# Four x tiles of an SSD group in one slot, and one POOL add of [128, 4, 128] where there were four of [128, 128]

## The chip, the core and the metric

The kernel runs on one NeuronCore of a Trainium2 chip. The metric is the device time of one execution in microseconds; the time quoted is the median of three runs. A profiled execution gives the trace, whose span starts at its first and ends at its last recorded instruction.

PE is the matmul engine (TensorE), DVE the vector engine, ACT the scalar engine, POOL the GpSimd engine; SP issues most DMAs. Each runs its own instructions strictly in order and waits on semaphores for the others.

## The reference, cut to what matters

One layer over 1024 rows of 1024 features: an RMS norm, a projection into eight parts, a gated MLP branch, a Mamba-2 branch (SSD), a merge, and an embedding stage. The change lies in the SSD branch, whose y is made of three parts:

```python
xs, bm, cm = jnp.split(silu(conv(xbc)), ...)            # x: 32 heads of 64; 4 groups of B and C
y_diag = einsum('bclsg,bclsgr,bcsgrp->bclgrp', CB, Lmat, Xdt)     # inside a chunk of 128 rows
y_off  = einsum('bcgrpn,bclgn,bclgr->bclgrp', prev, Cc, exp(dA_cs)) # from the state before the chunk
y = y_diag + y_off + X * d_skip
y_b = gated_group_rms_norm(y, z_b, ssm_norm_g)          # per group of 8 heads
```

## The kernel before

Everything is held transposed: features on partitions, the 1024 sequence positions along the free axis. Products that need fp32 accuracy are split into a high and a low part, so that a projection tile of 128 features (`in_proj`, by `mm3`, L107) is 48 matmuls of 128x512 into one of two PSUM slots `ps_...`.

The SSD branch runs over four groups of 8 heads. For a group, `group_in` makes the tiles B, C and four x tiles `cv_xs` by `conv_tile`: the projection, an ACT copy to SBUF (L343), three convolution steps on DVE that read the projection's PSUM slot (L346; the third one frees it), a tanh (L349) and a product (L350). Then come 8 chunks of 128 positions, `ssd_chunk`. In a chunk POOL fetches the decay rows (`lm`, L365), PE makes `pbc` and the transposes `pxt`; ACT turns `lm` into a decay matrix (L400, L401), DVE multiplies it by `cbm` (L402) and makes `xdt` and `dx` (L382, L386); ACT and POOL split `dx` into `dxh` (L391) and `dxl` (L392). PE then makes `pyd` (inside the chunk, L407), `pyo` (from the state, L412, from the second chunk on) and the new state `pst` (L425 to L427), which POOL and DVE add to the old one (L433, L436). DVE scales `pyo` into `ex` (L415), and for each of the four x tiles DVE forms x*d + `pyd` in place (L417), to which POOL adds `ex` (L420).

While the chunks of a group run, PE fills the time with the projections of the group's four z tiles (`zb`) and of the next group's B, C and x. After the last chunk `group_out` multiplies x by z on DVE (L449), squares on ACT (L450), sums three times (L454, on POOL except in the last group), splits the sum into `qa` (ACT, L458) and `qb` (POOL, L459), sums over partitions on PE (`pn`, L462 and L463) and scales x by the resulting `rs` on DVE (L467); four DMAs store it. `t_sums` (L480 to L484) puts eight POOL operations for a later stage behind four of the chunks. After the group loop the `ga` projections begin, opened by five matmuls `wipe` (L528).

The order of instructions is set by the Tile scheduler when the kernel is built: it lays the work out by its own simulated times, and a pool hands a new tile the slot that is free first. All tiles of [128, 1024] of this stage (the eight normalised input tiles `x0`, then B, C, x, z, `qa`, `qb`) are from one pool `big` of 15 slots (L62). So a change in the pools or in the length of an operation can move work on every engine.

Of the kernel before, what the change touches and what calls it, by code (L numbers as in the profile page):

```python
# [8 lines left out]
F32 = mybir.dt.float32  # L9
F32R = mybir.dt.float32r  # L10
AF = mybir.ActivationFunctionType
ALU = mybir.AluOpType

P = 128
S = 1024
D = 1024
# [8 lines left out]
O_U, O_V, O_ZA, O_ZB, O_XS, O_B, O_C, O_DT, O_GA, O_GB = (  # L25
    0, 1024, 2048, 3072, 5120, 7168, 7680, 8192, 8224, 9248)
# [3 lines left out]
def kernel(  # L30
# [8 lines left out]
    nc = tc.nc  # L39
# [13 lines left out]
    def phase_pool(name, bufs):  # L53
        return pools.enter_context(tc.tile_pool(name=name, bufs=bufs, reuse_waits="tile"))

    def phase_banks(name, bufs):
        return banks.enter_context(tc.tile_pool(name=name, bufs=bufs, reuse_waits="tile",
                                                space=bass.MemoryType.PSUM))

    t2 = phase_pool("t2", 2)  # L60
    small = phase_pool("small", 2)
    big = phase_pool("big", 15)  # L62
    pss = phase_banks("pss", 4)
    pmm = phase_banks("pmm", 2)

# [80 lines left out]
    rstd0 = const.tile([P, NCH], F32, name="rstd0")  # L146
    xt = []
    for t in range(NCH):
        xv = big.tile([P, D], F32, tag="big", name=f"x0_{t}")
        nc.sync.dma_start(out=xv, in_=x[t * P:(t + 1) * P, :])  # L150
        xt.append(xv)

# [16 lines left out]
    def vec(nm, i):  # L169
        c = offs[nm] + i  # L170
        return vT[:, c:c + 1]

    def cw(k, i):
        return cwT[:, k * 24 + i:k * 24 + i + 1]
# [21 lines left out]
    for hf in range(2):  # L196
# [13 lines left out]
        for k in range(KD):  # L210
            pt = ps_ss(f"pt0_{hf}_{k}")
            for i in range(4):
# [4 lines left out]
                in1=hhi[k][hf].bitcast(F32), op0=ALU.mult, op1=ALU.subtract)  # L217
# [24 lines left out]
    def in_proj(name, col):  # L242
        w = proj_w(name, col)
        ps = ps_mm(f"ps_{name}")
        for k in range(KD):
            hi, lo = w[k // 4]
            mm3(ps, hi[:, k % 4, :], lo[:, k % 4, :], hhi[k], hlo[k], k == 0, k == KD - 1)
        return flat(ps)
# [54 lines left out]
    for n in (15, 13, 11, 9, 7, 5, 3):  # L303
# [7 lines left out]
        in1=abc.unsqueeze(1).broadcast_to([P, NCH, NH]), op0=ALU.mult, op1=ALU.mult)  # L311
# [24 lines left out]
    tad = dram.tile([D, S], F32, name="tad")  # L336
    tbd = dram.tile([D, S], F32, name="tbd")

    def conv_tile(name, col, ci):

        ps = in_proj(name, col)
        a = big.tile([P, S], F32, tag="big", name=f"cv_{name}")
        act(a, ps, AF.Identity, scale=cw(3, ci), bias=vec("cb", ci))  # L343
        for k in (2, 1, 0):
            sh = 3 - k
            stt(out=a[:, sh:], in0=ps[:, :S - sh], scalar=cw(k, ci), in1=a[:, sh:],  # L346
                op0=ALU.mult, op1=ALU.add)
        th = t4.tile([P, S], F32, tag="t4", name=f"th_{name}")
        act(th, a, AF.Tanh, scale=0.5)  # L349
        stt(out=a, in0=th, scalar=1.0, in1=a, op0=ALU.add, op1=ALU.mult)  # L350
        return a

    def group_in(g):
        bT = conv_tile(f"B{g}", O_B + g * P, 16 + g)
        cT = conv_tile(f"C{g}", O_C + g * P, 20 + g)
        xs = [conv_tile(f"xs{g}_{j}", O_XS + (4 * g + j) * P, 4 * g + j) for j in range(4)]
        return xs, bT, cT

    def ssd_chunk(g, c, xs, bT, cT, hst):
        n = f"{g}_{c}"  # L360
        cl = slice(c * P, (c + 1) * P)
        hs = slice(g * HG, (g + 1) * HG)
# [16 lines left out]
        for j in range(4):  # L379
# [3 lines left out]
           in1=dth[:, c, hs].unsqueeze(2).broadcast_to([P, HG, HD]), op=ALU.mult)  # L383
        if not last:
            dx = t2.tile([P, HG, HD], F32, tag="dx", name=f"dx_{n}", bufs=1)
            tt(out=dx, in0=pxt.rearrange("s (r d) -> s r d", d=HD),  # L386
               in1=dec4[:, c, hs].unsqueeze(2).broadcast_to([P, HG, HD]), op=ALU.mult)
# [6 lines left out]
        if c > 0:  # L394
            ex = t2.tile([P, 4, P], F32, tag="ex", name=f"ex_{n}")
# [20 lines left out]
        for j in range(4):  # L416
            stt(out=xs[j][:, cl], in0=xs[j][:, cl], scalar=dcol[:, 4 * g + j:4 * g + j + 1],  # L417
                in1=pyd[:, j * P:(j + 1) * P], op0=ALU.mult, op1=ALU.add)
            if c > 0:
                nc.gpsimd.tensor_tensor(out=xs[j][:, cl], in0=xs[j][:, cl], in1=ex[:, j, :], op=ALU.add)  # L420

        if last:
            return None
# [8 lines left out]
        else:  # L432
            nc.gpsimd.tensor_tensor(out=hn, in0=hst,  # L433
                                    in1=cdec[:, c, hs].unsqueeze(2).broadcast_to([P, HG, HD]),
                                    op=ALU.mult)
# [3 lines left out]
    def z_tile(g, j):  # L439
        ps = in_proj(f"zb{g}_{j}", O_ZB + (4 * g + j) * P)  # L440
        a = big.tile([P, S], F32, tag="big", name=f"zb{g}_{j}")
        act(a, ps, AF.Tanh, scale=0.5)
        stt(out=a, in0=a, scalar=1.0, in1=ps, op0=ALU.add, op1=ALU.mult)
        return a
# [30 lines left out]
    def t_sums(k):  # L475
        a = t4.tile([P, S], F32, tag="t4", name=f"ta{k}")
        b = t4.tile([P, S], F32, tag="t4", name=f"tb{k}")
        b11, b12, b21, b22 = a[:, 0:512], a[:, 512:1024], b[:, 0:512], b[:, 512:1024]
        for o_, kk, h in ((b11, k, 0), (b12, k, 1), (b22, k + 4, 1), (b21, k + 4, 0)):
            ptt(out=o_, in0=hhi[kk][h].bitcast(F32), in1=hlo[kk][h].bitcast(F32), op=ALU.add)  # L480
        ptt(out=b11, in0=b12, in1=b11, op=ALU.subtract)
        ptt(out=b12, in0=b22, in1=b12, op=ALU.subtract)
        ptt(out=b22, in0=b22, in1=b11, op=ALU.subtract)
        ptt(out=b21, in0=b21, in1=b22, op=ALU.subtract)  # L484
        nc.sync.dma_start(out=td[k, 0], in_=a)
        nc.sync.dma_start(out=td[k, 1], in_=b)
# [7 lines left out]

    t_when = {(0, 4): 0, (1, 1): 1, (1, 5): 2, (2, 2): 3}
    cur = group_in(0)
    for g in range(G):
        xs, bT, cT = cur
        hst = None
        for c in range(NCH):  # L500
            hst = ssd_chunk(g, c, xs, bT, cT, hst)
            if (g, c) in t_when:
                t_sums(t_when[g, c])
        zs = [z_tile(g, j) for j in range(4)]
        if g + 1 < G:
            cur = group_in(g + 1)
            group_out(g, xs, zs)
# [9 lines left out]
    for j in range(2):  # L517
        ps = in_proj(f"ga{j}", O_GA + j * P)
        a = t4.tile([P, S], F32, tag="t4", name=f"ga{j}")
# [227 lines left out]
    def y_slots(pi, k, i):  # L747
        if pi == 0:
            return [g2.tile([P, 512], F32R, tag="T", name=f"y{i}0_{k}_{h}", bufs=24) for h in range(2)]
        if pi == 1:  # L750
            return [hp_.tile([P, 512], F32R, tag="hB", name=f"y{i}1_{k}_{h}") for h in range(2)]
        return two(big.tile([P, S], F32R, tag="big", name=f"y{i}{pi}_{k}"))

    for pi, (src, w, kp) in enumerate(parts):
        yh, yl = [], []
        if pi == 1:
# [3 lines left out]
            big = phase_pool("big", 15)  # L760
        for k in range(4):
# [3 lines left out]
            a, b = y_slots(pi, k, "h"), y_slots(pi, k, "l")  # L765
# [153 lines left out]
```

## Time and profile before

| | us |
|---|---|
| median of 3 runs (1490.16 to 1494.23) | 1493.08 |
| the profiled execution | 1492.43 |
| its span | 1490.7 |
| PE busy in the span | 1457.2 |
| DVE / ACT / POOL busy | 821.2 / 677.8 / 641.4 |

The span is 1.73 us shorter than the profiled execution's own time. By the trace, group 0's projections begin at about 50 us, the SSD chunks of the four groups run from 112 to 645 us, the `ga` tiles to 690, the pairs of projections of the gated branch to 1040, the output projections to 1390, and the embedding stage to the end. "Busy" of PE counts pipelined matmuls, which start some 0.23 us apart and last longer than that each; a bracket behind a row of a timeline gives the time for which the engine had nothing to run before it, and who released it.

### The profile page before, as it was taken

Reading aid. Unit: us, or ns where it says so; the run is one execution under the profiler, and the core shown is the slowest. Engines: PE = TensorE matmul, PEld = TensorE weight load, DVE = VectorE, ACT = ScalarE, POOL = GpSimd, SP = SyncE. Lnnn points to the kernel's source line nnn. Section 1 sums busy time; section 2 is a strip of 40 time slices with the busy share of each in tenths; the row PEclk is TensorE's granted clock in tenths of the full one; section 3 lists DMA queues with packets and bytes.
Section 4 is the critical chain, followed back from the end, with each engine's and each line's share of the span. In section 5 each row is a group of like instructions: output and inputs, shape, how many; then the busy total and the mean of one; then the engine's idle time right before and its main releaser. Section 6 shows DMA issues by size and latency. Waiting matters only on the chain.

```text
span 1490.7 us, 19028 instructions
## 1 busy us (share of the span) xinstructions
PE 1457.2 (98%) x7109; PEld 1199.7 (80%) x7109; DVE 821.2 (55%) x1214; ACT 677.8 (45%) x1216; POOL 641.4 (43%) x605
## 2 busy tenths in 40 slices
PE   6999999999999999999999999999999999999997
PEld 5788888778878888778888888888888888888885
DVE  5454566767666765575337646444133566932554
ACT  6453655365555645546444434344422221421544
POOL 1226555965686655645443445454332333100110
PEclk9999999999999999999999999999999999999999
DMA  8322222432142223235434242244432465633641
GB/s 279 109 75 84 73 84 57 132 110 86 57 142 85 71 77 108 86 136 196 128 106 134 87 134 83 74 128 148 131 118 98 142 207 166 196 122 127 226 184 57
DMA packets 134273, 180.42 MB, mean 121 GB/s; under 512 B 7348, under 2 KB 101764, under 8 KB 134180
## 3 DMA queue, kind: packets, MB, share of 16 engines
q1 hardware_dynamic: 116624, 116.54, 24.7%
q0 software_dynamic: 16464, 59.43, 11.8%
q10 hardware_dynamic: 1092, 3.23, 0.6%
q8 instruction: 56, 0.92, 0.3%
q14 instruction: 37, 0.30, 0.1%
HBM read 137.10 MB, written 42.07 MB: 120 GB/s over the span
## 4 chain that ended last, share of the span: by engine, by line
PE 88%; POOL 4%; DMA 2%; ACT 2%; issue 2%; DVE 1%; SPq 0%; DVEq 0%; ACTq 0%; POOLq 0%
PE po L107 18%; PE ps_xs L107 12%; PE ps_zb L107 8%; PE px L107 6%; PE ppg L107 6%; PE x_v L610 3%; PE ps_C L107 3%; PE x_za L610 3%; PE ps_ga L107 3%; PE x_u L610 3%; PE x_gb L610 3%; PE ps_B L107 2%; DMA lm<-csd 2%; PE pyd L407 2%; PE pyo L412 2%
## 5 line engine op out<-in xcount | busy, mean ns | idle before, releaser
L107 PE MATMUL po<-yh,hi_o 128*128 128x512 f32 x384 | 149.4, 389 | 0.0
L107 PE MATMUL po<-yl,hi_o 128*128 128x512 f32 x384 | 149.4, 389 | 0.0
L107 PE MATMUL po<-yh,lo_o 128*128 128x512 f32 x384 | 118.6, 389 | 0.0
L232 POOL TENSOR_TENSOR lo_o<-raw_o,hi_o 128x512 fp32r<-128x512 f32 x48 | 63.1, 1317 | 114.0 <-ACT hi_o L231 110.7
L107 PE MATMUL ps_zb<-hhi,hi_zb 128*128 128x512 f32 x256 | 101.1, 395 | 0.0
L107 PE MATMUL ps_zb<-hlo,hi_zb 128*128 128x512 f32 x256 | 100.8, 394 | 0.0
L107 PE MATMUL ps_xs<-hhi,hi_xs 128*128 128x512 f32 x256 | 100.6, 393 | 0.0
L107 PE MATMUL ps_xs<-hlo,hi_xs 128*128 128x512 f32 x256 | 100.2, 391 | 0.0
L420 POOL TENSOR_TENSOR cv_xs<-cv_xs,ex 128x128 f32<-128x128 f32 x112 | 78.6, 729 | 35.0 <-DVE ex L415 33.0
L231 ACT CAST hi_o<-raw_o 128x512 fp32r<-128x512 f32 x48 | 29.6, 622 | 135.5 <-PE po L107 108.4
L107 PEld LDWEIGHTS po<-yh,lo_o 128*128 128x128 f32 x384 | 72.1, 188 | 15.1
L107 PEld LDWEIGHTS po<-yh,hi_o 128*128 128x128 f32 x384 | 72.1, 188 | 14.9
L107 PEld LDWEIGHTS po<-yl,hi_o 128*128 128x128 f32 x384 | 72.0, 188 | 14.9
L400 ACT ACTIVATE lm<-lm,cs 128x128 f32<-128x128 f32 x256 | 79.4, 390 | 9.8 <-DMA lm<-csd 9.2
L107 PE MATMUL ps_zb<-hhi,lo_zb 128*128 128x512 f32 x256 | 81.4, 397 | 0.0
L346 DVE SCALAR_TENSOR_TENSOR cv_xs<-ps_xs,cwT,cv_xs 128x1023 f32<-128x1023 f32 (+2 forms) x48 | 61.5, 1281 | 35.0 <-ACT cv_xs L343 34.0
L107 PE MATMUL ps_xs<-hhi,lo_xs 128*128 128x512 f32 x256 | 79.3, 391 | 0.0
L398 ACT ACTIVATE ex<-lm 64x512 f32<-64x512 f32 x56 | 35.3, 630 | 93.4 <-DMA lm<-csd 55.5
L232 POOL TENSOR_TENSOR lo_zb<-raw_zb,hi_zb 128x512 fp32r<-128x512 f32 x32 | 48.6, 1519 | 58.6 <-ACT hi_zb L231 58.6
L792 DVE TENSOR_TENSOR m<-m,po 128x512 f32<-128x512 f32 x48 | 30.8, 684 | 64.0 <-PE po L107 63.9
L232 POOL TENSOR_TENSOR lo_xs<-raw_xs,hi_xs 128x512 fp32r<-128x512 f32 x32 | 42.5, 1329 | 54.4 <-ACT hi_xs L231 52.7
L768 DVE TENSOR_TENSOR yl<-yraw,yh 128x512 fp32r<-128x512 f32 x48 | 35.7, 778 | 45.6 <-ACT yh L767 44.2
(519 smaller groups left out, 4023.9 us busy)
## 6 DMA issues: line engine op xcount, KB each, us to landing
lm<-csd POOLq DMA_DIRECT2D x32, 512.0 KB, 4.1
raw_xs<-in_w_in_dram SPq DMA_DIRECT2D x16, 512.0 KB, 4.0
raw_zb<-in_w_in_dram SPq DMA_DIRECT2D x16, 512.0 KB, 4.1
ybd<-cv_xs SPq DMA_DIRECT2D x16, 512.0 KB, 3.0
yraw<-ybd POOLq DMA_DIRECT2D x16, 512.0 KB, 3.8
raw_o<-in_w_ob_dram SPq DMA_DIRECT2D x16, 512.0 KB, 3.5
gt<-tad POOLq DMA_DIRECT2D x16, 512.0 KB, 4.5
x<-in_x_dram SPq DMA_DIRECT2D x8, 512.0 KB, 7.5
```

Source lines behind the costliest of these rows:

```text
L107: nc.tensor.matmul(o_, lhsT=a, rhs=b[h], start=(first and h not in seen), stop=(last and cnt[h] == 3))
L231: nc.scalar.copy(out=hi, in_=raw)
L232: (lo_on or nc.gpsimd.tensor_tensor)(out=lo, in0=raw, in1=hi.bitcast(F32), op=ALU.subtract)
L346: stt(out=a[:, sh:], in0=ps[:, :S - sh], scalar=cw(k, ci), in1=a[:, sh:], op0=ALU.mult, op1=ALU.add)
L398: act(ex[h * HD:(h + 1) * HD], lv[h * HD:(h + 1) * HD, :, h, :], AF.Exp)
L400: act(lm[:, r_, :], lm[:, r_, :], AF.Relu, bias=cs[:, c, g * HG + r_:g * HG + r_ + 1], scale=-1.0)
L407: nc.tensor.matmul(pyd[h * HD:(h + 1) * HD, (r_ // 2) * P:(r_ // 2 + 1) * P], lhsT=xdt[:, r_, :], rhs=lm[:, r_, :], start=True, stop=True)
L412: nc.tensor.matmul(pyo[:, j * P:(j + 1) * P], lhsT=hst[:, 2 * j:2 * j + 2, :].rearrange("s r d -> s (r d)"), rhs=cT[:, cl], start=True, st ...
L420: nc.gpsimd.tensor_tensor(out=xs[j][:, cl], in0=xs[j][:, cl], in1=ex[:, j, :], op=ALU.add)
L610: nc.tensor.matmul(pst, lhsT=l_[:, k, :], rhs=r_, start=(first and k == 0 and n_ == 0), stop=(k == 3 and n_ == 2), skip_group_check=True)
L768: tt(out=b[h], in0=raw[:, hsl[h]], in1=a[h].bitcast(F32), op=ALU.subtract)
L792: tt(out=mj, in0=mj, in1=pf, op=ALU.add)
```

## The change

The four x tiles of a group become four planes of one tile of [128, 4, 1024] with a tag of its own and two slots; the eight input tiles `x0` use the same two slots at the start. The single slots fall from 15 to 7. With x in one tile, the four adds of a chunk become one POOL operation on [128, 4, 128], issued after all four DVE products of L417. Lines of the changed kernel lie 2 to 4 further down: the add is its L424, the products before it L421, the third convolution step L349, the products x*z L453.

```diff
-    big = phase_pool("big", 15)
+    big = phase_pool("big", 7)
...
-        xv = big.tile([P, D], F32, tag="big", name=f"x0_{t}")
+        if t % 4 == 0:
+            x4 = big.tile([P, 4, D], F32, tag="xs", name=f"x0_{t}", bufs=2)
+        xv = x4[:, t % 4, :]
...
-    def conv_tile(name, col, ci):
+    def conv_tile(name, col, ci, a=None):
...
-        a = big.tile([P, S], F32, tag="big", name=f"cv_{name}")
+        if a is None:
+            a = big.tile([P, S], F32, tag="big", name=f"cv_{name}")
...
+        x4 = big.tile([P, 4, S], F32, tag="xs", name=f"xs{g}", bufs=2)
+        xs = [conv_tile(f"xs{g}_{j}", O_XS + (4 * g + j) * P, 4 * g + j, x4[:, j, :]) for j in range(4)]
+        return x4, xs, bT, cT
...
         for j in range(4):
             stt(out=xs[j][:, cl], in0=xs[j][:, cl], scalar=dcol[:, 4 * g + j:4 * g + j + 1],
                 in1=pyd[:, j * P:(j + 1) * P], op0=ALU.mult, op1=ALU.add)
-            if c > 0:
-                nc.gpsimd.tensor_tensor(out=xs[j][:, cl], in0=xs[j][:, cl], in1=ex[:, j, :], op=ALU.add)
+        if c > 0:
+            nc.gpsimd.tensor_tensor(out=x4[:, :, cl], in0=x4[:, :, cl], in1=ex, op=ALU.add)
```

PE, DVE, ACT and SP run as many instructions as before; POOL has 84 fewer (28 adds for 112). But the schedule differs. On PE, this is the way from group 0 to group 1 before, from the last chunk's `pyd_7` on (48 matmuls each for the x tiles 1, 2 and 3 of the next group, then z; the sum over partitions `pn` of the old group):

```order
L407 MATMUL pyd_7_1506<-lm_7_1480,xdt_7_1491 64x128 x8
L412 MATMUL pyo_7_1515<-cv_C_737,hst_6_1477 128x128 x4
L107 MATMUL ps_xs_1_1988<-hlo_0_208,hi_xs_1_0_1980 128x512
...
L107 MATMUL ps_xs_2_2055<-hhi_0_190,hi_xs_2_0_2047 128x512
...
L107 MATMUL ps_xs_3_2122<-hhi_0_190,hi_xs_3_0_2114 128x512
...
L107 MATMUL ps_zb_0_2750<-hhi_0_190,hi_zb_0_0_2742 128x512
...
L462 MATMUL pn_0_2195<-qa_2191,onesr 128x512
L462 MATMUL pn_1_2199<-qa_2191,onesr 128x512
L368 MATMUL pbc_0_2214<-cv_C_1903,cv_B_1836 128x128
```

And this is the same place after the change:

```order
L411 MATMUL pyd_7_1479<-lm_7_1453,xdt_7_1464 64x128 x8
L416 MATMUL pyo_7_1488<-cv_C_731,hst_6_1450 128x128 x4
L107 MATMUL ps_xs_1_1958<-hhi_0_184,hi_xs_1_0_1950 128x512
...
L107 MATMUL ps_xs_2_2024<-hhi_0_184,hi_xs_2_0_2016 128x512
...
L466 MATMUL pn_0_2162<-qa_2158,onesr 128x512
L466 MATMUL pn_1_2166<-qa_2158,onesr 128x512
L372 MATMUL pbc_0_2181<-cv_C_1873,cv_B_1806 128x128
L384 MATMUL pxt_0_2190<-ident,xs_1881 128x128
L107 MATMUL ps_xs_3_2090<-hhi_0_184,hi_xs_3_0_2082 128x512
```

Between `pyo_7` and `pn` there were 41 + 48 + 48 + 30 = 167 projection matmuls; there are 96. The same holds from group 1 to 2 and from 2 to 3.

On DVE, at the same place, before (the third step of L346 on the next group's x tile 0 is the one that reads 128x1021; it stands ahead of the four products x*z of the old group):

```order
L346 SCALAR_TENSOR_TENSOR cv_xs_0_1970<-ps_xs_0_1921,cwT,cv_xs_0_1970 128x1022
L415 TENSOR_TENSOR ex_7_1493<-pyo_7_1515,ex_7_1493 128x512
L346 SCALAR_TENSOR_TENSOR cv_xs_0_1970<-ps_xs_0_1921,cwT,cv_xs_0_1970 128x1021
L449 TENSOR_TENSOR cv_xs_0_804<-cv_xs_0_804,zb_0_1588 128x1024
L449 TENSOR_TENSOR cv_xs_1_871<-cv_xs_1_871,zb_1_1650 128x1024
```

And after:

```order
L419 TENSOR_TENSOR ex_7_1466<-pyo_7_1488,ex_7_1466 128x512
L349 SCALAR_TENSOR_TENSOR xs_1881<-ps_xs_0_1892,cwT,xs_1881 128x1023
L349 SCALAR_TENSOR_TENSOR xs_1881<-ps_xs_0_1892,cwT,xs_1881 128x1022
L453 TENSOR_TENSOR xs_739<-xs_739,zb_0_1558 128x1024
L453 TENSOR_TENSOR xs_739<-xs_739,zb_1_1620 128x1024
L453 TENSOR_TENSOR xs_739<-xs_739,zb_2_1682 128x1024
L453 TENSOR_TENSOR xs_739<-xs_739,zb_3_1744 128x1024
L349 SCALAR_TENSOR_TENSOR xs_1881<-ps_xs_0_1892,cwT,xs_1881 128x1021
```

All four products now stand ahead of the third step. The third place is ACT at the end of group 3, ahead of its last chunk. Before:

```order
L400 ACTIVATE lm_7_5077<-lm_7_5077,cs 128x128 x8
L375 CAST bh_6_5017<-pbc_6_5012 128x128
L231 CAST hi_ga_1_5738<-raw_ga_5732 128x512
L391 CAST dxh_6_5030<-dx_6_5028 128x512
L520 ACTIVATE ga_5495<-ps_ga_5446 128x1024
L401 ACTIVATE lm_7_5077<-lm_7_5077 128x1024
```

After:

```order
L404 ACTIVATE lm_7_4978<-lm_7_4978,cs 128x128 x8
L233 CAST hi_ga_1_5636<-raw_ga_5630 128x512
L524 ACTIVATE ga_5393<-ps_ga_5344 128x1024
L379 CAST bh_6_4921<-pbc_6_4916 128x128
L405 ACTIVATE lm_7_4978<-lm_7_4978 128x1024
L395 CAST dxh_6_4934<-dx_6_4932 128x512
```

The two operands of `pst_6`, `bh_6` and `dxh_6`, have moved back behind `ga`, and `dxh_6` behind the exponential of the last chunk too. At the start of the kernel, PE now runs 48 matmuls of the embedding product `pple` (four of its tiles) ahead of the first transposes of `x0`, which stood among them before.

## Rows read from the trace of the kernel before

**Rows 1.** Page of the profile: busy time by engine; shares of the chain that ended last.
```profile
PE 1457.2 (98%) x7109; PEld 1199.7 (80%) x7109; DVE 821.2 (55%) x1214; ACT 677.8 (45%) x1216; POOL 641.4 (43%) x605
...
PE 88%; POOL 4%; DMA 2%; ACT 2%; issue 2%; DVE 1%; SPq 0%; DVEq 0%; ACTq 0%; POOLq 0%
```

**Rows 2.** Windows: stretch, length; busy us (instructions) of PE, PEld, DVE, ACT, POOL; clock.
```profile
112.00:645.00 533.00, 524.39 (x2846) 428.63 (x2845) 337.71 (x452) 289.03 (x548) 339.89 (x315) 0.99 0.29 90
...
645.00:690.00 45.00, 45.00 (x200) 37.19 (x199) 29.60 (x30) 25.76 (x40) 14.52 (x10) 1.00 0.58 199
...
635.00:640.00 5.00, 3.69 (x22) 2.67 (x23) 3.44 (x5) 0.00 (x0) 2.89 (x5) 0.50 0.57 211
```

**Rows 3.** Waits of PE: line, what released it: us in total, times, longest.
```profile
PE ptp L182 <- DMA ptm<-in_p_dram: 10.1, 2, 5.5
PE pyd L407 <- DVE lm L402: 3.1, 2, 1.8
PE pt L213 <- DVE hlo L216: 2.6, 1, 2.6
PE pst L425 <- ACT dxh L391: 1.7, 1, 1.7
PE pst L426 <- POOL dxl L392: 1.7, 1, 1.7
PE pyd L407 <- DVE xdt L382: 1.6, 2, 0.8
```

**Rows 4.** Timeline of PE: start, us, instruction, [idle before it, releaser].
```profile
227.74 1.16 PE L412 MATMUL pyo<-cv_C,hst 128*128 128x128 f32 x8
...
306.83 1.09 PE L407 MATMUL pyd<-lm,xdt 128*64 128x128 f32 x16 [1.84 <-DVE lm L402]
...
637.22 1.97 PE L407 MATMUL pyd<-lm,xdt 128*64 128x128 f32 x16 [1.31 <-DVE lm L402]
639.12 2.08 PE L412 MATMUL pyo<-cv_C,hst 128*128 128x128 f32 x8
```

**Rows 5.** Groups of POOL by shape: count, busy us, mean ns, idle before.
```profile
L420 POOL TENSOR_TENSOR cv_xs<-cv_xs,ex 128x128 f32<-128x128 f32 x112 | 78.6, 729 | 35.0 <-DVE ex L415 33.0 <-PE wipe L528 2.0
...
L392 POOL TENSOR_TENSOR dxl<-dx,dxh 128x512 fp32r<-128x512 f32 x28 | 37.3, 1333 | 39.8 <-ACT dxh L391 37.5 <-PE ps_xs L107 2.3
...
L433 POOL TENSOR_TENSOR hst<-hst,cdec 128x512 f32<-128x512 f32 x24 | 25.4, 1057 | 5.2 <-DVE hst L436 3.5 <-ACT hst L431 1.1 <-PE pxt L380 0.4
```

**Rows 6.** Timeline of DVE, POOL and ACT from group 0 to group 1.
```profile
232.07 1.27 DVE L346 SCALAR_TENSOR_TENSOR cv_xs<-ps_xs,cwT,cv_xs 128x1021 f32<-128x1021 f32 x1
233.26 6.14 DVE L449 TENSOR_TENSOR cv_xs<-cv_xs,zb 128x1024 f32<-128x1024 f32 x4
...
246.66 2.42 POOL L454 TENSOR_TENSOR zb<-zb,zb 128x1024 f32<-128x1024 f32 x1
...
261.42 1.04 ACT L458 CAST qa<-zb 128x1024 fp32r<-128x1024 f32 x1
...
272.88 9.10 DVE L467 SCALAR_TENSOR_TENSOR cv_xs<-cv_xs,vT,rs 128x1024 f32<-128x1024 f32 x4 [2.34 <-ACT rs L465]
```

**Rows 7.** Timeline of POOL and DVE: four adds alone, and beside another product.
```profile
301.40 1.71 POOL L420 TENSOR_TENSOR cv_xs<-cv_xs,ex 128x128 f32<-128x128 f32 x4
...
302.51 4.17 DVE L402 TENSOR_TENSOR lm<-lm,cbm 128x1024 f32<-128x1024 f32 x1 [2.20 <-ACT lm L401]
...
586.69 2.70 POOL L420 TENSOR_TENSOR cv_xs<-cv_xs,ex 128x128 f32<-128x128 f32 x4 [1.47 <-DVE ex L415]
...
587.43 1.22 DVE L402 TENSOR_TENSOR lm<-lm,cbm 128x1024 f32<-128x1024 f32 x1
```

**Rows 8.** Timeline of ACT and DVE before the last chunk of group 3.
```profile
631.27 0.61 ACT L391 CAST dxh<-dx 128x512 fp32r<-128x512 f32 x1
...
632.71 1.04 ACT L401 ACTIVATE lm<-lm 128x1024 f32<-128x1024 f32 x1
...
633.78 3.29 DVE L402 TENSOR_TENSOR lm<-lm,cbm 128x1024 f32<-128x1024 f32 x1
```

More of the change, by code (lines that the diff above doesn't have):

```diff
@@ L355, in group_in, with ssd_chunk @@
         cT = conv_tile(f"C{g}", O_C + g * P, 20 + g)
-        xs = [conv_tile(f"xs{g}_{j}", O_XS + (4 * g + j) * P, 4 * g + j) for j in range(4)]
-        return xs, bT, cT
-    def ssd_chunk(g, c, xs, bT, cT, hst):
+        x4 = big.tile([P, 4, S], F32, tag="xs", name=f"xs{g}", bufs=2)
+        xs = [conv_tile(f"xs{g}_{j}", O_XS + (4 * g + j) * P, 4 * g + j, x4[:, j, :]) for j in range(4)]
+        return x4, xs, bT, cT
+    def ssd_chunk(g, c, x4, xs, bT, cT, hst):
         n = f"{g}_{c}"
@@ L497 @@
     for g in range(G):
-        xs, bT, cT = cur
+        x4, xs, bT, cT = cur
         hst = None
         for c in range(NCH):
-            hst = ssd_chunk(g, c, xs, bT, cT, hst)
+            hst = ssd_chunk(g, c, x4, xs, bT, cT, hst)
             if (g, c) in t_when:
```

## Prediction, made before the changed kernel had run

> **What bounds the kernel now.** I read the page's busy times and chain first, then the waits of PE, then PE by stretches. PE is busy for 1457.2 of 1490.7 us, and 88% of the chain that ended last is its own work [rows 1]; POOL has 4% of the chain and 43% of the span. PE's instructions are the same before and after, so the change can only touch the 33.5 us in which PE is idle, and the rate at which PE runs. In the whole SSD stage, 533 us, PE is idle for 533.0 - 524.4 = 8.6 us [rows 2]. The waits that make this up are few [rows 3]: 3.1 us for the decay product `lm` (twice), 1.7 for `dxh`, 1.7 for `dxl`, 1.6 for `xdt` (twice). None names the four adds of L420. Outside the stage, 10.1 us are waits for the first input and 2.6 for the first normalised tile [rows 3]; the rest lies mostly behind the last matmul, where the change moves nothing.
>
> **The POOL operation itself.** Today's 112 adds take 78.6 us, 0.73 each on average [rows 5]. The trace has no POOL operation on [128, 4, 128]; the nearest rows with as many elements are L392 (128x512, two full inputs, 1.33 us) and L433 (128x512, one input broadcast, 1.06 us) [rows 5]. I take 1.33 as nearest in its operands: 28 x 1.33 = 37.2 us, 41 us less POOL time (44 to 49 at 1.06, less if the new operation is held up as the old ones are). On the path this is worth nothing by itself: the adds start when DVE's `ex` arrives (33.0 of the 35.0 us that POOL idled before them [rows 5]), and their last reader is `group_out`, a group's end later. Four adds alone take 1.71 us and beside a DVE product 2.70 [rows 7]; one operation for four is therefore at best some 0.4 to 1.4 us earlier for whatever POOL does next, mostly the state update (L433) that has a whole chunk to spare. I put it at 0 on the path.
>
> It can also hurt there. At 586.69 the four adds ran 2.70 us while the product L402, begun at 587.43, took 1.22; at 302.51 the same product took 4.17 with POOL at work beside it [rows 7]. So one of the two engines waits, and which of them changes. [...]
>
> **The group boundaries.** Here the schedule moves most, three times. First, `pn` comes 96 matmuls behind `pyo_7` instead of 167. A projection matmul costs 45.00/200 = 0.225 us [rows 2], so PE arrives 96 x 0.225 = 21.6 us after `pyo_7`. In the trace `pyo_7` began at 227.74 and lasts about 0.9 without its drain; the third sum ended at 246.66 + 2.42 = 249.08; with `qa` at 1.04 behind it, 250.1 [rows 4, 6]. PE would arrive at 227.74 + 0.9 + 21.6 = 250.2: a margin of 0.1 us by the old duration. In the new order the products x*z start one step (1.27 us) earlier and the four adds end earlier, so I expect a margin of one to five us and a cost of 0. The gain is that `group_out` gets done earlier: its 9.10 us of L467 on DVE [rows 6] stood just ahead of the next group's `xdt`, and that is the `xdt` wait of 2 x 0.8 us [rows 3]. In the new order 83 projection matmuls lie between the last `pn` and the next `pyd_0`, before it was 54: 6.5 us more cover. So I take the whole **1.6 us** as gained. Of the `lm` wait at 306.83 (1.84 us [rows 4]) a part goes too, since the row shows POOL and DVE working through the same backlog; I take half, **0.9 us**, between 0 and 1.8.
>
> Second, DVE's third convolution step on the next x tile 0 is now behind the four products. It frees the PSUM slot that x tile 2 needs, 48 matmuls = 10.8 us after `pyo_7`: at 227.74 + 0.9 + 10.8 = 239.4. The first two steps were over at 232.07; 6.14 us of products give 238.2, the step itself 1.27 [rows 6]: 239.5. So PE is stalled for 0.1 us if the products run as in the trace. If they run as L467's four did, 9.10 us, since POOL's sums now start beside them, it is 3.0 us; a faster run gives 0. I take **0.35 us** each, nearest to the row of the same instruction, 1.0 us in all, and keep 0 to 9.0 for the range.
>
> **The start.** PE runs 48 `pple` matmuls ahead of the x transposes that stood among them, which fills the gap before the second input, then waits longer for the same `hlo` (2.6 us today [rows 3]). The chain that ends this wait, norm and transposes of the first four x tiles, has the same work, and PE has done the same work when it ends: 0. The longer idle stretch (about 4.7 us, as the `pple` work done earlier leaves a hole) is the ground for rival **B**.
>
> **The end of group 3.** Between chunk 6 and chunk 7 PE waits 1.7 for `dxh`, 1.7 for `dxl` and 1.31 for `lm` [rows 3, 4]. Afterwards ACT runs `ga` (1.0 us) and the exponential (1.04) ahead of `dxh`: from 631.27 it goes to about 633.3, 2 us later, and `pst_6` with it. `pbc_7` and `pxt_7` stand behind the first `pst_6` on PE, so the decay product of chunk 7, which began at 633.78, now waits for `pbc_7`, to about 634.9. But it took 3.29 us there beside POOL's `dxl` and adds [rows 8]; with one POOL operation in their place I expect 1.3 to 2.2. `xdt_7` then comes behind it (0.7), so `pyd_7` starts at 636.9 to 637.8, against 637.22 today: -0.3 to +0.6. I take **+0.4**. In this stretch the granted clock is 0.50 [rows 2], after PE had mostly waited since 630: `pyd` takes 1.97 us for 1.09, `pyo` 2.08 for 1.16 [rows 4]. PE waits there in the new order too, so I leave the clock as it is.
>
> **The slots.** Seven single slots hold B, C, four z and one tile ahead; the next group's C must wait for one of them. The order has its copy out of PSUM in the same place as before, behind `dxh_6`, so nothing is drawn later; 0.
>
> **Sum.** -1.6 - 0.9 + 1.0 + 0.4 = -1.1 us, from the profiled 1492.43 (0.65 below the median of its runs, and inside their 4 us): **1491.3 us**. That is no change: 0.3%, about what a measurement of this kernel can tell, is 4.5 us, or 1488.6 to 1497.6 around the median.
>
> **Rivals.** **A, the stage runs dry of waits.** Shorter POOL work lets all the SSD waits go, the ones at the end of group 3 as well (8.1 us in rows 3 without the start), and with them the clock drop, some 0.9 us on `pyd` and as much on `pyo` [rows 4]. That is up to 9.9 us, 1482.5; with the tail's waits only partly gone, about 1486. Against it: the waits of the tail hang on the decay rows' way through ACT and on PE having nothing else to run, not on the adds. 0.11.
>
> **B, the start loses the clock.** If the hole of 4.7 us before the first tile brings the half clock as the idle stretch at 630 to 635 did [rows 2], the next matmuls run at half rate; at the tail about 5 us ran so, losing 2.5 to 3.5. Time: 1491.3 + 3 = 1494.3. Against: the hole of 2.6 us today changes nothing that the trace shows. 0.17.
>
> **C, slower: DVE becomes late at the boundaries.** POOL's longer operations hold DVE's two-input products, so that the four products take 9.1 us rather than 6.1; the third convolution step then comes 3.0 us late for x tile 2 at each of the three boundaries, and PE stands. By the margins above this decides as soon as the products need more than about 6.1 us. Price 3 x 3.0 = 9.0 less the 1.0 counted: 1491.3 + 8.0 = 1499.3. For it: the margin of 0.1 us, and 4.17 us for one product at 302.51 [rows 7]. Against: POOL's sums can only start when the second square is done, so at most the last two products run beside them. At one boundary alone it is 1494. 0.15.
>
> **D, it doesn't do what it says.** The new operation takes as long as the four adds (2.7 us): POOL saves little, nothing else moves, as POOL is not on the path; this is inside the forecast's own range.
>
> **How the numbers follow.** The forecast (with D) has 0.57, its own range 1488.5 to 1495.0. The range for 8 in 10, 1487 to 1498, takes in B and C where it strikes once or twice; it leaves out most of A (0.09) and C at all three (0.09). Faster by over 0.3%: A 0.11 and 0.04 of the forecast, 0.15. Slower by over 0.3%: C's 0.10 at full price, 0.02 of B and 0.03 of waits that I have not seen, 0.15. Within 0.3%: 0.70.
>
> **What would show it.** In the profile after: 28 rows of the add at about 1.3 us and POOL near 600 us; no `xdt` wait of PE at 283 and 424, and a `lm` wait below 1.84 near 307; PE before the first matmul of the x tile 2 of groups 1 to 3 idle for less than 0.7 us (C: about 3), and none before `pn`; one wait of about 4.7 us for `hlo` at the start with full clock behind it (B: half clock); the clock still 0.5 near 637. The forecast is wrong if PE's idle time in the SSD stage leaves 5 to 12 us, or if the projections themselves run at another pace.

## The result, and the profile after

The changed kernel takes 1502.17 us (1500.22 to 1506.86), the kernel before 1493.55 in the same comparison: a ratio of 1.0065, interval 1.005 to 1.008. It is slower by 8.6 us, where no change was forecast, and 4.2 us above the upper end of the range. The profiled execution is the longest of the four (1506.86 us, span 1505.1); a second one, the run after_again, took 1504.55 and is read beside it.

The first line of the page, after:

```profile
PE 1462.3 (97%) x7109; PEld 1202.8 (80%) x7109; DVE 810.4 (54%) x1214; ACT 677.2 (45%) x1216; POOL 617.2 (41%) x521
```

Against [rows 1] POOL is down by 24 us and DVE by 11, and PE is up by 5.1 us for the same matmuls. PE is idle for 1505.1 - 1462.3 = 42.8 us, before it was 33.5. So 9.3 of the 14.4 us between the two profiled spans are waits and 5.1 are a slower clock (mean granted clock 0.992, before 0.996). (The medians differ by 8.6: this execution of the changed kernel was a long one.) Of the 9.3 us, 0.9 lie ahead of 50 us, 5.5 in the SSD stage up to 650 (14.1 idle for 8.6), 2.6 right behind it and 0.3 behind 1390. The waits of PE (what waited, on what; us in total, times, longest), to be held against [rows 3]:

```profile
PE pyd L411 <- DVE xdt L386: 6.0, 5, 2.5
PE ptp L184 <- DMA ptm<-in_p_dram: 5.5, 1, 5.5
PE pt L215 <- DVE hlo L218: 4.5, 1, 4.5
PE x_v L614 <- ACT a_v L622: 3.2, 2, 2.6
PE pple L107 <- ACT pple L227: 3.1, 1, 3.1
PE pn L466 <- ACT qa L462: 2.8, 2, 1.9
PE pst L429 <- ACT dxh L395: 2.7, 3, 2.4
```

The wait for `xdt` has grown from 1.6 to 6.0 us, and five kinds are new or larger: `qa` (2.8), `pple` at the start (3.1), `hlo` (4.5 for 2.6), `a_v` of the stage behind the groups (3.2, in the trace before 0.6), `dxh` (2.7 for 1.7). Two are gone: the second wait for the first input (`ptm`, 4.6 of 10.1 us) and `lm` (3.1). Part of the growth of `xdt` is this `lm` under another name. At the place where PE waited 1.84 us for `lm` [rows 4] it now waits 2.46 for `xdt`, because DVE makes `xdt` behind the product L406 instead of ahead of it (DVE and PE):

```profile
304.42 3.80 DVE L406 TENSOR_TENSOR lm<-lm,cbm 128x1024 f32<-128x1024 f32 x1 [7.15 <-ACT lm L405]
308.14 0.68 DVE L386 TENSOR_TENSOR xdt<-pxt,dth 128x512 f32<-128x512 f32 x1
...
308.97 1.89 PE L411 MATMUL pyd<-lm,xdt 128*64 128x128 f32 x16 [2.46 <-DVE xdt L386]
```

`xdt` and `lm` together went from 4.7 to 6.0 us. The clock, by windows of 2 us (busy us and instructions by engine, then the granted clock):

```profile
32.00:34.00 2.00, 1.62 (x7) 1.43 (x8) 2.00 (x4) 0.65 (x2) 0.00 (x0) 0.66 0.68 271
...
310.00:312.00 2.00, 2.00 (x14) 1.67 (x11) 1.32 (x6) 1.95 (x6) 1.91 (x2) 0.50 0.03 8
...
398.00:400.00 2.00, 2.00 (x6) 1.54 (x5) 2.00 (x1) 1.36 (x2) 2.00 (x2) 0.50 0.00 0
...
648.00:650.00 2.00, 1.85 (x16) 1.57 (x16) 0.69 (x2) 0.00 (x0) 0.00 (x0) 0.50 0.03 4
```

At a granted clock of 0.50 PE works in four places; before, the trace had one ahead of the last matmul, at the end of group 3 [rows 2]. In each of the four, PE had just waited 1.9 to 4.5 us, with little work between.

The operation itself, by POOL's groups (instructions, busy us, mean ns, idle before):

```profile
L424 POOL TENSOR_TENSOR xs<-xs,ex 128x512 f32<-128x512 f32 x28 | 40.5, 1448 | 21.8 <-DVE ex L419 21.5
...
L437 POOL TENSOR_TENSOR hst<-hst,cdec 128x512 f32<-128x512 f32 x24 | 39.3, 1637 | 6.1 <-DVE hst L440 4.7 <-ACT hst L435 1.0 <-PE pxt L384 0.4
```

28 operations of 1.45 us take 40.5 us where the four adds took 78.6 [rows 5]. But the state's product (L437, L433 before) has gone from 25.4 to 39.3 us: it is now the POOL operation that runs beside DVE's decay product, and takes over the delay that the adds had (four of them 2.70 us at 586.69 for 1.71 at 301.40 [rows 7]). By the timelines 16 of its 24 rows overlap a product L406, at 1.93 us on average, and the other 8 take 1.04; before, one of the 24 overlapped.

### The profile page after: what moved, and what is told of

It is laid out like the page before. It is cut to its first block, busy times and chain, and to the rows that moved or that the text cites. A ratio compares the mean times of both kernels' runs of the same rounds, so it can differ in the third digit from the quotient of the medians.

```text
span 1505.1 us, 18935 instructions
## 1 busy us (share of the span) xinstructions
PE 1462.3 (97%) x7109; PEld 1202.8 (80%) x7109; DVE 810.4 (54%) x1214; ACT 677.2 (45%) x1216; POOL 617.2 (41%) x521
## 4 chain that ended last, share of the span: by engine, by line
PE 85%; ACT 4%; DMA 3%; DVE 3%; POOL 2%; issue 2%; SPq 0%; DVEq 0%; ACTq 0%; POOLq 0%
PE po L107 17%; PE ps_zb L107 9%; PE ps_xs L107 7%; PE px L107 6%; PE ppg L107 6%; PE ps_B L107 3%; PE ps_C L107 3%; PE x_za L614 3%; PE x_u L614 3%; PE x_gb L614 3%; PE x_v L614 3%; PE ps_ga L107 2%; PE pyd L411 2%; PE pyo L416 2%; DMA lm<-csd 1%
## 5 line engine op out<-in xcount | busy, mean ns | idle before, releaser
L404 ACT ACTIVATE lm<-lm,cs 128x128 f32<-128x128 f32 x256 | 78.7, 389 | 7.8 <-DMA lm<-csd 7.2
L402 ACT ACTIVATE ex<-lm 64x512 f32<-64x512 f32 x56 | 35.3, 630 | 98.0 <-DMA lm<-csd 83.1
L234 POOL TENSOR_TENSOR lo_xs<-raw_xs,hi_xs 128x512 fp32r<-128x512 f32 x32 | 46.3, 1447 | 80.2 <-ACT hi_xs L233 78.3
L349 DVE SCALAR_TENSOR_TENSOR xs<-ps_xs,cwT,xs 128x1023 f32<-128x1023 f32 (+2 forms) x48 | 61.4, 1279 | 20.7 <-ACT xs L346 19.9
L421 DVE SCALAR_TENSOR_TENSOR xs<-xs,dcol,pyd 128x128 f32<-128x128 f32 x128 | 35.8, 342 | 44.2 <-PE pyd L411 44.2
```

The source lines that it names most:

```text
L234: (lo_on or nc.gpsimd.tensor_tensor)(out=lo, in0=raw, in1=hi.bitcast(F32), op=ALU.subtract)
L402: act(ex[h * HD:(h + 1) * HD], lv[h * HD:(h + 1) * HD, :, h, :], AF.Exp)
L404: act(lm[:, r_, :], lm[:, r_, :], AF.Relu, bias=cs[:, c, g * HG + r_:g * HG + r_ + 1], scale=-1.0)
```

## The experiments

Two theories went into them. **O**: the slots of the change make the scheduler write another order, and the order makes the waits; the operation is worth about nothing. **P**: the operation costs, since it waits for all four products, runs longer in one piece and holds DVE (4.17 us for one product beside POOL's work [rows 7]). Orders were held by edges between neighbours on an engine's queue; such an edge orders the issue and is meant to add no wait:

```python
for e, o in order.items():                  # a recorded order for each engine
    ...                                     # l: the instructions of engine e
    for a, b in zip(o, o[1:]):
        tc.add_manual_dep(l[b], l[a].name, dep, reason="order")     # dep: of the kind NoSync
```

| kernel | slots | POOL adds | order | us | ratio to before (interval) |
|---|---|---|---|---|---|
| after | 7 + 2 of four | one | its own | 1502.17 | 1.0065 (1.005 to 1.008) |
| slots_only | 7 + 2 of four | four | its own | 1507.64 | 1.0093 (1.0073 to 1.0112) |
| split_slots | 7 + 8 | four | its own | 1507.01 | 1.0092 (1.0069 to 1.0115) |
| old_order_one | 7 + 2 of four | one | before's | 1498.26 | 1.0030 (1.002 to 1.0039) |
| old_order_four | 7 + 2 of four | four | before's | 1498.89 | 1.0042 (1.0027 to 1.0057) |
| after_order_four | 7 + 2 of four | four | after's | 1509.74 | 1.0106 (1.0089 to 1.0123) |
| four_order_one | 7 + 2 of four | one | slots_only's | 1499.49 | 1.0045 (1.0026 to 1.0064) |
| pn_late | 7 + 2 of four | one | one rule | 1500.82 | 1.0046 (1.0031 to 1.0061) |
| x0_half | 7 + 2 of four | one | its own | 1512.39 | 1.0124 (1.0107 to 1.0141) |
| tuned | 15 | four | before's, edited | 1496.15 | 1.0017 (1.0007 to 1.0027) |
| tuned2 | 15 | four | before's, edited | 1489.97 | 0.9971 (0.9961 to 0.9981) |

**The old order with the new operation, and with the four adds.** Seven single slots cannot take the old order whole: the convolution of C of groups 2 and 3 had to be left free.

```diff
+        _in_order(tc, _mybir)   # the kernel before's order; old_order_one: after.py, old_order_four: slots_only
```

> The changed kernel (x in one tile, one POOL operation for four), but every engine is held to the order of the kernel before by issue-order edges that add no wait; only the convolution of C of groups 2 and 3 is left free, since seven single slots cannot take it as early as before. Theory O (the loss is the new order, the operation itself is worth about nothing): 1490 to 1495 us, PE idle in the SSD stage 7 to 10 us as before. Theory P (the loss is the operation, which waits for all four products, runs longer in one piece and holds DVE): 1499 to 1504 us with new xdt and lm waits of PE.

> The slots of the change (x in tiles of four, seven single slots) and the old order as in old_order_one, but with the four POOL adds of before: the only difference from old_order_one (1498.26 us) is the operation itself. Theory O (the operation is worth about nothing, the slots cost the time): 1497 to 1500 us, with the same wait of 2.6 us for the convolution of C of group 2 behind the last use of B. Theory P (the operation costs): 1493 to 1496 us. If the operation gains: 1500 to 1504 us.

1498.26 and 1498.89 us: 4 us of the 8.6 go with the order, 5 stay, and the operation makes no difference (their intervals overlap). The first lies above theory O's 1490 to 1495 and below theory P's 1499 to 1504; the second was expected so. What stays comes with the slots. The trace of old_order_one, ACT and PE:

```profile
363.88 1.21 ACT L346 ACTIVATE cv_C<-ps_C,vT,cwT 128x1024 f32<-128x1024 f32 x1 [4.18 <-PE pbc L372]
...
370.10 0.67 PE L107 MATMUL ps_xs<-hhi,hi_xs 128*128 128x512 f32 x1 [2.58 <-DVE cv_C L349]
```

The copy of C of group 2 out of PSUM waits 4.18 us for `pbc`, the last use of the old group's B: it needs B's slot. The projection of x tile 1, which needs the PSUM slot that C's convolution frees, then waits 2.58 us, and goes on at a granted clock of 0.55 (370 to 372 us), its first matmuls 0.47 and 0.43 us apart. The trace of old_order_four has the same wait, 2.60 us. Neither stands in [rows 3]. With `a_v` (2.0 us for 0.6) this is most of the 4.5 us by which PE is idle longer than before (1497.6 - 1459.6 = 38.0 for 33.5). No run holds the kernel before to its own order unchanged, so what the edges cost by themselves is read from other runs: tuned2 below, held in the same way, is faster than before.

**The slots alone.** slots_only is the change with the four adds kept; split_slots leaves every tile as before and only divides the 15 slots into eight for x and seven for the rest.

```diff
-    big = phase_pool("big", 15)
+    big = phase_pool("big", 7)
...
-        a = big.tile([P, S], F32, tag="big", name=f"cv_{name}")
+        a = big.tile([P, S], F32, tag="xs", name=f"cv_{name}", bufs=8) if name[0] == "x" else \
+            big.tile([P, S], F32, tag="big", name=f"cv_{name}")
```

> The slots of the change (x and x0 in tiles of four, seven single slots) with the four POOL adds of before; the scheduler is free. Theory O: the order is again a new one (pn 96 matmuls behind pyo_7, pple ahead of the x transposes), so 1498 to 1504 us with the same kinds of waits as the changed kernel (hlo about 4.5 us with half clock behind it, qa, xdt). Theory P: 1491 to 1496 us.

> The kernel before with its 15 slots divided into eight for x (and x0) and seven for the rest; every x tile is still a tile of its own and the four POOL adds stay. The order it gets is nearly that of slots_only. Theory O (the division of the slots makes the loss): 1502 to 1509 us as slots_only, with its waits for qa and xdt, but without the 1.6 to 2.6 us wait for a_v if that comes from the release of a whole tile of four. Theory P, or a loss by the tile of four alone: 1491 to 1496 us.

Both come to 1507 us (slots_only above the 1498 to 1504 that theory O gave it), and their orders differ in a few rows only (`pn` 96 matmuls behind `pyo_7` in both). So dividing the slots is enough for the whole loss, and more: 14 us, with the waits of the changed kernel. Waits of PE in split_slots:

```profile
PE pyd L408 <- DVE xdt L383: 8.4, 4, 3.5
...
PE pn L463 <- ACT qa L459: 6.5, 3, 2.7
...
PE pt L213 <- DVE hlo L216: 2.9, 1, 2.9
...
PE pple L107 <- ACT pple L225: 2.3, 1, 2.3
```

One wait grows with tiles of four. In the changed kernel the first operand sum of the stage behind the groups, which takes over memory of the closed pools, waits for the store of the x tile (DVE and PE):

```profile
685.64 0.69 DVE L594 TENSOR_TENSOR s_v<-s_v,raw_v 128x512 f32<-128x512 f32 x1 [5.86 <-DMA ybd<-xs]
...
706.73 0.73 PE L614 MATMUL x_v<-T,hi_s_v 128*128 128x512 f32 x2 [2.63 <-ACT a_v L622]
```

With single x tiles, in split_slots, PE's wait at that place is 0.32 us:

```profile
707.88 0.73 PE L611 MATMUL x_v<-T,hi_s_v 128*128 128x512 f32 x2 [0.32 <-ACT a_v L619]
```

It was 1.6, 1.4 and 1.2 in slots_only, old_order_one and old_order_four, 2.6 and 3.3 in the two profiles of the changed kernel. DVE waits for a store of x in split_slots too, but 2.89 us, where slots_only has 4.75. This fits a tile of four that comes free only with the last of its stores; no run shows that by itself.

**The operation, in the new orders.** The two new orders were each held and given the other form of the add.

```diff
+        _in_order(tc, _mybir)   # after_order_four: slots_only with after.py's order; four_order_one: the reverse
```

> The changed kernel's order on every engine, held by issue-order edges, with four POOL adds in the place of the one operation. With four_order_one, slots_only and the changed kernel itself it separates the operation from the order that comes with it. If the 5.5 us between slots_only (1507.6) and the changed kernel (1502.2) are the operation's: 1505 to 1509 us. If they are the order's: 1501 to 1504 us.

> The order of slots_only on every engine, with the one POOL operation where the last of the four adds stood. If the 5.5 us are the operation's: 1500 to 1503 us. If they are the order's: 1505 to 1509 us.

In the changed kernel's order, four adds take 1509.74 us and one operation 1502.17; in slots_only's, 1507.64 and 1499.49. By these medians the operation is worth 7.6 and 8.2 us, by the ratios of the table, each against the kernel before in its own comparison, 6 and 7. Both runs lie just beyond the ranges expected if the 5.5 us were the operation's. The held order stands on the side of the four adds in the first pair and on the side of the one operation in the second, so a cost of holding would raise one difference and lower the other; they hardly differ. Theory O falls in this part: only in the old order is the operation worth nothing. The waits of PE that it shortens, in after_order_four,

```profile
PE pn L466 <- ACT qa L462: 4.2, 2, 2.3
...
PE pst L429 <- ACT dxh L395: 3.0, 3, 2.6
...
PE pst L430 <- POOL dxl L396: 1.9, 3, 0.8
```

and with one operation in the same order, in after_again:

```profile
PE pn L466 <- ACT qa L462: 1.8, 2, 1.1
...
PE pst L429 <- ACT dxh L395: 2.4, 3, 2.0
...
PE pst L430 <- POOL dxl L396: 0.6, 1, 0.6
```

That is 4.3 us; the whole idle time of PE falls by 6.1 (1508.7 - 1464.9 = 43.8 to 1502.8 - 1465.1 = 37.7). Against the first profile of the changed kernel it is only 2.0 us in these rows and 1.0 of idle time (42.8), and 2.6 us of clock; so two profiles of one kernel do not settle which waits carry the gain. The other pair agrees on `qa`: 5.6 us in slots_only, 2.3 in four_order_one, with 42.0 and 37.4 us of idle time. `dxl` is POOL's own, and `qa` follows POOL's third sum; that POOL is on PE's way in the new orders fits these rows, where [rows 3] has it there once.

**One rule for `pn`, and the start.** pn_late puts `pn` of groups 0 to 2 behind the last projection matmul of x tile 3; x0_half gives four of the input tiles slots of their own.

```diff
+            with tc.issue_after(xs3_mm) if g + 1 < G else nullcontext():   # pn_late, around the pn matmuls
...
+        if t == 4:                                                         # x0_half
+            x4 = big.tile([P, 4, D], F32, tag="xs", name=f"x0_{t}", bufs=2)
+        xv = x4[:, t % 4, :] if t >= 4 else big.tile([P, D], F32, tag="big", name=f"x0_{t}")
```

> The changed kernel with one more rule for the order: the four pn matmuls of groups 0 to 2 stand behind the last projection matmul of the next group's x tile 3 (144 matmuls behind pyo_7, where the changed kernel has 96 for the qa part). Theory O: the two waits for qa (2.8 us) and the half clock behind one of them (about 1.8) go, 2 to 5 us less than the changed kernel, 1497 to 1500 us. Theory P: no change from 1502.

> The changed kernel with the first four input tiles x0 in single slots of their own, the other four in one tile of four. The order of the start is then near that of before. Theory O: no wait of 4.5 us for hlo and no half clock behind it, 2 to 3 us less, 1499 to 1500 us, if the groups keep their order. Theory P: no change from 1502.

pn_late, 1500.82, lies 1.4 us below the changed kernel and above the 1497 to 1500 expected, and the intervals of the two overlap: in its trace the `qa` waits are gone and `xdt` is at 3.5 us, but `bh` (1.3) and `dxl` (2.8) came up. That settles little. x0_half missed: the scheduler put the x transposes of both halves of the sequence ahead of `pple`, and with nothing to fill, PE waited six times between 20 and 35 us and worked at a granted clock of 0.50 from 34 to 36 us. PE in x0_half:

```profile
32.08 1.97 PE L215 MATMUL pt<-ident,x 128*128 128x128 f32 x8 [4.14 <-DVE hlo L218]
...
34.00:36.00 2.00, 1.29 (x7) 1.11 (x7) 1.45 (x2) 0.78 (x2) 0.00 (x0) 0.50 0.00 0
```

**The two kernels once more.**

> The kernel before, once more with a profile: whether the wait of about 2.6 us for hlo at the start is followed by the half clock (as it was in old_order_one, where the order there is the same) or by the full clock (as in the first profile). Theory O: 1490 to 1496 us, the waits in the SSD stage as in the first profile; the start may show either clock.

> The changed kernel once more with a profile: which of its waits are there every time. Theory O: the waits set by the order stay (hlo about 4.5 and pple about 3 us at the start, qa 0.9 and 1.9, xdt 2.5 near 309, dxh 2.4 at the end of group 3, a_v 2.6), the half clock at the start and behind the waits near 309 and 397 may come or go, by up to 2 us each: 1500 to 1507 us.

The waits of the kernel before repeat to 0.8 us or better. Those of the changed kernel are all there again, but repeat only to about 1.6 us: in after_again `xdt` is 5.5 (for 6.0), `a_v` 3.9 (3.2), `hlo` 2.9 (4.5), `pple` 2.0 (3.1), `qa` 1.8 (2.8). Where they stand belongs to the order; how long they last does so only in part. Nor does the half clock repeat: the place near 398 us is gone and there are others, near 22 and 705 us (0.50 from 22 to 24 and from 704 to 706 us). The last section has more on the start.

**Edits of the old order.** If the order decides, the kernel before can gain by a few moves. tuned keeps its slots and operations and moves the work around three of its waits; tuned2 takes one of the moves back and adds `bl`.

```text
 DVE, groups 1, 2:   L467 x1, [xdt, dx, (tuned2: bl)], L467 x3          (was: L467 x4, xdt, dx, ..., bl)
 POOL, tuned only:   fetch of lm, chunk 2 of group 1, ahead of L483      (was: 5 operations later)
 end of group 3, PE: pxt_6, ga x10, pyd_6, pyo_6, pst_6 and pxt_7, ga x12, pyd_7   (was: ga x22 ahead of pyd_6)
 end of group 3:     bh_6, dxh_6, dxl_6 forward; ga's tanh behind the last exponential
```

> The kernel before, slots and operations unchanged, held to its own order except at four places: xdt and dx of the first chunk of groups 1 and 2 stand behind the first of the four products L467 instead of the fourth; the fetch of the decay rows of chunk 2 of group 1 stands ahead of two sums of POOL; and at the end of group 3 the last 22 ga matmuls are spread (10 ahead of pyd_6, 12 between chunk 6 and chunk 7), with bh_6, dxh_6 and dxl_6 moved forward and ga behind the exponential of chunk 7. Theory O (the order of a few instructions decides the waits): the xdt waits (1.6 us), the lm wait of 1.8 us, and most of the 4.8 us and the half clock at the end of group 3 (about 2.7) go: 1483 to 1488 us. Theory P says nothing; if those waits are only pushed on to the next instruction, 1491 to 1494 us.

> As the run tuned, but the fetch of the decay rows stays where the kernel before has it, and bl of the first chunk of groups 1 and 2 moves forward together with xdt and dx. In tuned one product L402 on DVE ran 13.3 us while POOL worked through ten operations without a pause (from 287.8 to 300.0), which cost PE 7.6 us and about 2.5 more by the half clock behind it. If that came from the moved fetch alone: the 7.6 us and its half clock are gone, the lm wait of 1.8 us is back, the bl wait of 1.0 us is gone, so 1496.2 - 7.6 - 2.5 + 1.8 - 1.0 = 1486.9 us, and 1485 to 1489 as the range. If the early xdt is what let POOL run through, the product stays above 5 us and the time above 1491.

tuned took 1496.15, where theory O gave 1483 to 1488: the waits at the end of group 3 fell from 4.8 to 1.6 us, and the moved fetch cost more than that. DVE, POOL and PE in tuned:

```profile
287.79 13.27 DVE L402 TENSOR_TENSOR lm<-lm,cbm 128x1024 f32<-128x1024 f32 x1
...
287.83 1.31 POOL L483 TENSOR_TENSOR tb<-tb,ta 128x512 f32<-128x512 f32 x1
...
298.94 1.03 POOL L433 TENSOR_TENSOR hst<-hst,cdec 128x512 f32<-128x512 f32 x1
...
301.20 1.12 PE L407 MATMUL pyd<-lm,xdt 128*64 128x128 f32 x8 [7.63 <-DVE lm L402]
```

One decay product on DVE ran for 13.27 us while POOL worked without a pause through ten operations, from the second row to the third, and PE waited 7.63 us for it. With the fetch back in its place, tuned2 takes 1489.97 us, ratio 0.9971 (0.9961 to 0.9981): faster than both kernels, by 4.2 and 12 us. I had expected 1486.9, and 1485 to 1489 as the range, so it is outside by 1 us; the rows show the difference as a longer `lm` wait (2.4 for 1.8) and a new `xdt` wait of 2.0 us at the end of group 3. Page and waits of PE in tuned2:

```profile
PE 1454.0 (98%) x7109; PEld 1197.5 (81%) x7109; DVE 817.8 (55%) x1214; ACT 677.8 (46%) x1216; POOL 637.5 (43%) x605
```

```profile
PE pyd L407 <- DVE lm L402: 3.4, 2, 2.4
...
PE pyd L407 <- DVE xdt L382: 2.0, 1, 2.0
...
PE pst L426 <- POOL dxl L392: 1.1, 2, 0.6
```

PE is busy 3.2 us less than in [rows 1], for the same matmuls: this execution has no half clock before the last matmul.

## Why the prediction was wrong, point by point

**What bounds the kernel**: right. PE's idle time and clock account for the whole difference. The forecast's sum, -1.1 us, was a price for PE's idle time alone; it became 9.3 us, and the SSD stage was idle for 14.1, outside the 5 to 12 that the forecast gave as its sign.

**The POOL operation**: the duration was near (1.45 us, expected 1.33), the saving too large (24 us, expected 41), since the state's product became longer by 13.9 us. "On the path nothing" holds in the old order (1498.26 to 1498.89) and is wrong in the order that the kernel has, where it is 6 to 8 us. I read its worth from the old trace, in which no wait of PE names POOL but one.

**The slots, at 0, and the order that came with them, at -1.1**: this is the step that failed. I looked where the order has the copy of C, found it where it was, and took the slots as free; the new order, which I had in front of me, I priced at the boundaries, the start and the end of group 3 as a small gain. Dividing the slots costs 14 us with the order that it leads to, and 5 us in the old order, where the copy's wait for B's slot reaches PE. In the changed kernel the copy waits for the same `pbc`, and no wait of PE hangs on it (ACT):

```profile
363.51 1.21 ACT L346 ACTIVATE cv_C<-ps_C,vT,cwT 128x1024 f32<-128x1024 f32 x1 [2.41 <-PE pbc L372]
```

So here the slots cost by way of the order, in the terms that follow, and by the late x tile behind the groups (2.6 us for `a_v`), which the sum did not have.

**The group boundaries**: the forecast took a gain of 1.6 us on `xdt` and 0.9 on `lm`, and `pn` with one to five us in hand. Measured, `xdt` still costs 1.9 us at the boundaries (0.43 and 1.46, before 2 x 0.8), the `lm` wait of 1.84 has become one of 2.46 for `xdt`, and `pn` costs 2.8. The steps for `pn` and `xdt` failed in the same way: I followed the producer of each operand and not the queue of the engine that it runs on. ACT, POOL and PE of the changed kernel, from group 0 to 1:

```profile
235.46 1.29 ACT L402 ACTIVATE ex<-lm 64x512 f32<-64x512 f32 x2 [6.08 <-DMA lm<-csd]
...
240.60 2.94 ACT L454 ACTIVATE zb<-xs 128x1024 f32<-128x1024 f32 x3
...
248.81 2.41 POOL L458 TENSOR_TENSOR zb<-zb,zb 128x1024 f32<-128x1024 f32 x1
...
251.25 1.04 ACT L462 CAST qa<-zb 128x1024 fp32r<-128x1024 f32 x1 [3.70 <-POOL zb L458]
...
252.35 0.74 PE L466 MATMUL pn<-qa,onesr 128*128 128x512 f32 x2 [0.88 <-ACT qa L462]
```

The products x*z were done at 237.7, sooner than I had reckoned. But the squares stand on ACT behind `ex` of the next group, and ACT stood 6.08 us for the fetch of its decay rows, until 235.46. Before, it stood there too, 5.33 us, but only until 233.35. Then seven decay steps (L404, 2.14 us) stand between the first and the second square, and POOL's split `lo_zb` between the second and the third sum took 2.28 us for 1.30. The third sum ended at 251.22, before at 249.08, and PE waited 0.88 us for `qa`, 1.92 at the next boundary. The count of 96 matmuls, given for all three boundaries, holds at these two, and for the half of `pn` that reads `qa`; the other half comes 144 behind `pyo_7`. At the third boundary all of `pn` stands 144 behind, and PE does not wait for it. For `xdt`, from group 1 to 2:

```profile
410.25 0.63 PE L467 MATMUL pn<-qb,onesr 128*128 128x512 f32 x2
...
415.84 1.06 ACT L352 ACTIVATE th_xs<-xs 128x1024 f32<-128x1024 f32 x1 [3.97 <-DVE xs L349]
...
418.21 1.27 ACT L468 ACTIVATE rs<-pn,eps 128x512 f32<-128x512 f32 x2
...
422.39 8.66 DVE L471 SCALAR_TENSOR_TENSOR xs<-xs,vT,rs 128x1024 f32<-128x1024 f32 x4 [4.23 <-ACT rs L469]
...
431.71 1.09 PE L411 MATMUL pyd<-lm,xdt 128*64 128x128 f32 x16 [1.46 <-DVE xdt L386]
```

`pn` was done at 410.9, but the logarithm stands behind the tanh of x tile 3, which waits for DVE, and a table load of 1.28 us: it began at 418.2, and the four L471 ended at 431.05. `xdt` behind them made PE wait 1.46 us. The 6.5 us of cover that I had counted went into ACT's queue. The 1.0 us taken for the third convolution step came out by luck: x tile 2 waits at no boundary. PE's 1.05 us under L349 is x tile 3 at the third boundary (539.80 us), which waits for all three steps on x tile 1; they ran from 535.74 to 539.66, after DVE had stood 6.21 us for ACT's copy.

**The end of group 3**: its waits come to 4.9 us (before 4.8), as forecast.

**The start and the clock**: 0 was wrong for the start; 0.9 us more idle, and some 3.4 us at half clock between 32 and 36 us (rival B, which was priced at 3 us; by the trace the matmuls of `pple` start 0.43 us apart there and 0.23 behind it, so I estimate their cost at about 1.7). The forecast left the clock as it was elsewhere. In the profiled execution it is low in three places more than before, and costs 5.1 us more.

**Rival C** gives 1499.3 us, near the result, by a mechanism that did not occur: the four products took 4.62 us where it needed 9.1. That the number is near is luck.

What stays open: why the scheduler, given divided slots, writes that order; and which rows make up what the operation is worth in the new orders. How the 8.6 us of the medians divide into waits and clock is known for the profiled executions alone.

## What to carry to other kernels

Where a scheduler and its pools set the order, a change of slots is a change of the whole order: dividing a pool of 15 into 7 and 8, with no instruction changed, cost 14 us here, while the operation that it was made for gained 0 to 8, by the order. Test it in parts (slots alone, operation alone, old order held), and cost a moved instruction by everything that its engine's queue has ahead of it, not by its operands. A held order is also a tool: a few moves in the old one, with slots and operations unchanged, gained 4 us (tuned2), after a first set had lost 3 (tuned).

## What the runs showed of the hardware

**A DVE product against a run of POOL operations.** In tuned the product L402 ended at 301.06 us, 1.09 us after the last of ten POOL operations that followed each other without a gap (298.94 + 1.03 = 299.97). The product of [rows 7] at 302.51 ended at 306.68, and the POOL operations beside it at 305.60, 1.08 earlier. The shortest of the 32 rows of this product in the trace of the kernel before is 1.21 us. So by the rows these two products were done only when POOL had paused, about 1.1 us after its last operation. It is not always so. In the kernel before, another product L402 took 1.88 us and ended at 288.14 while POOL's rows left no gap, and the POOL operation beside it was longer by about 1 us than its usual 1.3 [rows 5] (DVE, POOL):

```profile
286.26 1.88 DVE L402 TENSOR_TENSOR lm<-lm,cbm 128x1024 f32<-128x1024 f32 x1
...
287.02 2.27 POOL L392 TENSOR_TENSOR dxl<-dx,dxh 128x512 fp32r<-128x512 f32 x1
```

What decides between the two is not shown.

**The clock at the start.** In before_again PE waited 2.58 us for `hlo` and went on at full clock:

```profile
32.34 0.66 PE L213 MATMUL pt<-ident,x 128*128 128x128 f32 x4 [2.58 <-DVE hlo L216]
...
32.00:34.00 2.00, 1.66 (x10) 1.45 (x11) 2.00 (x4) 1.00 (x2) 0.00 (x0) 1.00 0.93 360
```

In old_order_four, with the same order there, it waited 2.57 us and went on at half:

```profile
32.10 1.11 PE L215 MATMUL pt<-ident,x 128*128 128x128 f32 x4 [2.57 <-DVE hlo L218]
...
32.00:34.00 2.00, 1.90 (x7) 1.71 (x8) 2.00 (x5) 0.77 (x2) 0.00 (x0) 0.50 1.04 408
```

The same wait ended on either side here, which is worth 1 to 2 us in these rows and is part of the 1 to 8 us by which executions of one kernel differ here.
